# A cross-entropy gradient kernel on one core: whole-block and row transfers change places

## The chip, the core and the metric

The kernel runs on 1 core of one Trainium2 chip. The time is device microseconds of one execution. Four kinds of workers matter here:

- VectorE (DVE in the profile) and ScalarE (ACT) compute on rows that lie in SBUF.
- SyncE (SP) computes nothing; it issues the loads, each when what it waits for is done.
- 16 DMA engines move data between HBM and SBUF. SP and ACT each have a queue on all 16 of them: in the profile q1 is SP's and q10 is ACT's.
- TensorE (PE) and GpSimd (POOL) are used in the first microseconds only.

An instruction of an engine waits until a semaphore has reached a count, and raises one when it ends. A DMA raises its semaphore when its data has landed.

## The reference

For each of 8 x 1024 = 8192 positions there are 8192 float32 logits and one label. The output is the softmax minus the one-hot vector of the label:

```python
logits_max = np.max(logits, axis=-1, keepdims=True)
exp_logits = np.exp(logits - logits_max)
softmax = exp_logits / np.sum(exp_logits, axis=-1, keepdims=True)
one_hot[batch_idx, seq_idx, labels] = 1.0
return (softmax - one_hot).astype(np.float32)
```

Logits (268 MB) are read once and the output (268 MB) is written once.

## The kernel before

**Tiling.** A "row" `t` of the program is a tile of 128 positions, one on each of the 128 SBUF partitions, with 8192 float32 on each: 32 KB per partition, 4.19 MB in all. There are T = 64 rows, numbered from 0. Two rows make a block (G = 2), so B = 32 blocks; block `b` has rows `2b` and `2b+1`. In HBM the two rows of a block lie side by side for each partition, 64 KB in one piece. The tile X in SBUF has three slots (SLOTS = 3) of one block each; block `b` lives in slot `b % 3`, is computed in place there, and is stored from there.

**Steps of a row.** All are written with the helper `run` (its line 76 stands for nearly every instruction in the profile).

- `row_max`: DVE takes the negated maximum of the row (`m <- X`).
- `exponentials`: ACT computes exp(x - max) in place and the sum into `s` (`X <- X,m`, and a short instruction that reads the sum).
- `mark`: two ACT instructions (`away`, then `hot`) put a one-hot row, as bytes, into PSUM. A PSUM buffer is free again when the row two before has been finished.
- `finish`: DVE takes the reciprocal of the sum, and then computes row x reciprocal - one-hot in place (`X <- X,r,hot`). The last row's is cut into two column halves.
- `store`: ACT's queue issues the DMA to HBM.

**Order of the main loop.** For block `b` with rows t0 and t1, DVE runs: maximum of t1, finish of t0, maximum of the next block's first row, finish of t1. The third of these is the look-ahead; it is there when `ORDER[b + 1]` is "r", which holds for every block. ACT runs: exponentials of t1, store of t0, marks of row t0 + 2, exponentials of the next block's first row, store of t1, marks of row t1 + 2. At the end of a turn of the loop SP is given the loads of block `b + 3`. The engines run these lists in order and wait where the semaphores say so.

**Pieces.** Two strings give one letter for each block. `LOADS`: "s" loads each row in two halves of the partitions, one by SP and one by ACT; "r" loads row by row with SP; "w" loads the block with one DMA of SP. `STORES`: "r" stores each row when it is finished. A load waits only for those stores of the block before in its slot that it overlaps (`meets`): a row load for the store of the same row, a whole load for both, and a row load for a whole store if the block was stored whole. Before the change blocks 0 to 2 are loaded as "s", 3 and 4 by rows, 5 to 28 whole, 29 to 31 by rows, and all blocks are stored by rows.

**The end.** After the last block ACT waits until the stores of the last three blocks have landed.

Of the kernel before, what the change touches and what calls it, by code (L numbers as in the profile page):

```python
# [7 lines left out]
P = 128  # L8
G = 2
SLOTS = 3  # L10

LOADS = "sssrrwwwwwwwwwwwwwwwwwwwwwwwwrrr"
STORES = "rrrrrrrrrrrrrrrrrrrrrrrrrrrrrrrr"
ORDER = "rrrrrrrrrrrrrrrrrrrrrrrrrrrrrrrr"


@with_exitstack
def kernel(
# [6 lines left out]
    nc = tc.nc  # L25
# [10 lines left out]
    N, V = x_nv.shape  # L36
    T = N // P
# [4 lines left out]
    o_b = o_nv.rearrange("(b p j) v -> b p j v", p=P, j=G)  # L42
# [4 lines left out]
    X = const.tile([P, SLOTS, G, V], fp32)  # L47
# [16 lines left out]
    with tc.tile_critical():  # L64
        sem = tc.alloc_semaphore
        got = [[sem(f"got{i}{q}") for q in range(4)] for i in range(SLOTS)]
        put = [[sem(f"put{i}{q}") for q in range(4)] for i in range(SLOTS)]
# [3 lines left out]
        def run(engine, waits, counter, method, **operands):  # L71

            waits = list(dict.fromkeys(waits))
            for w in waits[:-1]:
                engine.wait_ge(*w)  # L75
            instruction = getattr(engine, method)(**operands)  # L76
            for w in waits[-1:]:
                instruction._wait_ge(*w)
            step = 16 if method == "dma_start" else 1
            instruction.then_inc(counter, step)  # L80
            count[counter.name] = count.get(counter.name, 0) + step
            return counter, count[counter.name]

        every, rows = slice(0, P), slice(0, G)
        one = [slice(j, j + 1) for j in range(G)]
        halves = [slice(i, P, 2) for i in range(2)]
        quarters = [slice(i, P, 4) for i in range(4)]
        PIECES = {
            "r": [(every, js) for js in one],
            "s": [(ps, js) for js in one for ps in halves],  # L90
            "w": [(every, rows)],
            "h": [(ps, rows) for ps in halves],
            "q": [(ps, rows) for ps in quarters],
        }

        def meets(a, b):
            sets = [[set(range(*d.indices(n))) for d, n in zip(p, (P, G))] for p in (a, b)]
            return all(x & y for x, y in zip(*sets))

        loaded, stored = {}, {}  # L100
        maxed, summed, marked, finished, freed = {}, {}, {}, {}, {}

        def load(b):
            loaded[b] = []
            before = stored.get(b - SLOTS, [])
            for q, piece in enumerate(PIECES[LOADS[b]]):
                ps, js = piece
                free = [w for other, w in before if meets(piece, other)]
                queue = nc.scalar if LOADS[b] == "s" and ps == halves[1] else nc.sync
                w = run(  # L110
# [5 lines left out]
        def store(t):  # L116
            b, j = divmod(t, G)
            stored.setdefault(b, [])
            for q, piece in enumerate(PIECES[STORES[b]]):
                ps, js = piece  # L120
                if js.stop != j + 1:
                    continue
                w = run(
                    nc.scalar, [finished[t]], put[b % SLOTS][q], "dma_start",
                    out=o_b[b, ps, js, :], in_=X[ps, b % SLOTS, js, :],
                )
                stored[b].append((piece, w))

        def row(t):
            return X[:, t // G % SLOTS, t % G, :]  # L130
# [4 lines left out]
        def row_max(t):  # L135
            b, j = divmod(t, G)
            arrived = {w[0].name: w for piece, w in loaded[b] if meets(piece, (every, one[j]))}
            maxed[t] = run(
                nc.vector, arrived.values(), dve, "tensor_reduce",
                out=m[:, t : t + 1], in_=row(t), axis=mybir.AxisListType.X, op=Alu.max, negate=True,  # L140
            )

        def exponentials(t):
            w = run(
                nc.scalar, [maxed[t]], act, "activation",
                out=row(t), in_=row(t), func=Act.Exp, bias=m[:, t : t + 1], scale=1.0,
                accum_out=s[:, t : t + 1],
            )
            summed[t] = w

        def mark(t):
            if t >= T:
                return
            w = run(
                nc.scalar, ([made] if t < G else [freed[t - G]]) + ([marked[t - 1]] if t else []), act, "activation",
                out=away[:], in_=count16[:], func=Act.Abs, bias=at(word, t), scale=1.0,
            )
            marked[t] = run(
                nc.scalar, [w], act, "activation",
                out=hot[:, t % G, :], in_=away[:], func=Act.Relu, bias=at(unit, t), scale=at(minus, t),  # L160
            )

        def finish(t, n=1):
            w = run(nc.vector, [summed[t]], dve, "reciprocal", out=r[:, t : t + 1], in_=s[:, t : t + 1])
            bytes_ = hot[:, t % G, :].bitcast(u8)
            for i in range(n):
                c = slice(i * V // n, (i + 1) * V // n)
                last = run(
                    nc.vector, [marked[t], w] if i == 0 else [], dve, "scalar_tensor_tensor",
                    out=row(t)[:, c], in0=row(t)[:, c], scalar=r[:, t : t + 1], in1=bytes_[:, c],  # L170
                    op0=Alu.mult, op1=Alu.subtract,
                )
            finished[t] = freed[t] = last

        w_raw = run(nc.scalar, [], lab_got, "dma_start", out=lab_raw[:], in_=lab_bp)
        for b in range(SLOTS):
            load(b)
        w = run(nc.gpsimd, [], pool, "memset", ap=ident[:], constant=0.0)
        w_ident = run(
            nc.gpsimd, [w], pool, "affine_select",  # L180
            out=ident[:], in_=ident[:], compare_op=Alu.not_equal, fill=1.0,
# [8 lines left out]
        for j in range(G):  # L190
            w = run(
                nc.tensor, [w_ident, w_lab], pe, "transpose",
                out=lab_ps[:, j, :], in_=lab_f[:, j, :], identity=ident[:],
            )
        w = run(nc.vector, [w], dve, "tensor_copy", out=lab[:], in_=lab_ps)
        w = run(
            nc.vector, [w], dve, "tensor_scalar",
            out=part[:], in0=lab[:], scalar1=2, scalar2=None, op0=Alu.arith_shift_right,
        )
        w_word = run(  # L200
            nc.vector, [w], dve, "tensor_scalar",
            out=word[:], in0=part[:], scalar1=-1.0, scalar2=None, op0=Alu.mult,
        )
        w = run(
            nc.vector, [w_word], dve, "tensor_scalar",
            out=lab[:], in0=lab[:], scalar1=3, scalar2=None, op0=Alu.bitwise_and,
        )
        w = run(
            nc.vector, [w], dve, "tensor_copy", out=minus[:], in_=lab[:]
        )  # L210
        powers = [256.0**k for k in range(4)]
        w = run(
            nc.vector, [w], dve, "tensor_scalar",
            out=unit[:], in0=minus[:], scalar1=0.0, scalar2=powers[0], op0=Alu.is_equal, op1=Alu.mult,
        )
        for k in (1, 2, 3):
            w = run(
                nc.vector, [w], dve, "tensor_scalar",
                out=part[:].bitcast(fp32), in0=minus[:], scalar1=float(k),
                scalar2=powers[k], op0=Alu.is_equal, op1=Alu.mult,  # L220
            )
            w = run(
                nc.vector, [w], dve, "tensor_tensor",
                out=unit[:], in0=unit[:], in1=part[:].bitcast(fp32), op=Alu.add,
            )
        made_dve = run(
            nc.vector, [w], dve, "tensor_scalar",
            out=minus[:], in0=unit[:], scalar1=-1.0, scalar2=None, op0=Alu.mult,
# [8 lines left out]
        for b in range(B):  # L237
            t0, t1 = b * G, b * G + 1
            nxt = t1 + 1
            if ORDER[b] == "b":  # L240
                if t0 not in maxed:
                    row_max(t0)
                    exponentials(t0)
                row_max(t1)
                exponentials(t1)
                finish(t0)
                store(t0)
                mark(t0 + G)
                finish(t1)
                store(t1)  # L250
                mark(t1 + G)
                if b + SLOTS < B:
                    load(b + SLOTS)
                continue
            if t0 not in maxed:
                row_max(t0)
                exponentials(t0)
            row_max(t1)
            finish(t0)
            exponentials(t1)  # L260
            store(t0)
            mark(t0 + G)
            ahead = nxt < T and ORDER[b + 1] == "r"
            if ahead:
                row_max(nxt)
            finish(t1, 1 if t1 + 1 < T else 2)
            if ahead:
                exponentials(nxt)
            store(t1)
            mark(t1 + G)  # L270
            if b + SLOTS < B:
                load(b + SLOTS)
# [33 lines left out]
```

## Time and profile before

| | us |
|---|---|
| median of 3 runs (1248.36 to 1248.45) | 1248.44 |
| the profiled execution | 1248.19 |
| its span in the trace | 1246.4 |
| DVE busy | 1120.1 (90%) |
| ACT busy | 722.7 (58%) |
| one maximum, DVE, x64 | 8.68 |
| one finish of a whole row, DVE, x63 | 8.75 |
| one half of the last row's finish, DVE, x2 | 4.48 |
| one row of exponentials, ACT, x64 | 7.12, and 0.19 for the sum |
| `away` and `hot`, ACT, x64 each | 2.00 and 2.06 |
| one reciprocal, DVE, x64 | 0.15 |
| mean rate of all DMA over the span | 431 GB/s |

How to read the lines that follow. A page line of an engine gives busy time and share of the span. The DMA line cuts the span into 40 slices, 9 for 90% busy or more. A queue line gives packets, megabytes and the time of its packets as a share of 16 engines over the stretch asked for; it counts a packet in full where it starts, so that a short stretch can show over 100%. Packets of 4 bytes that raise semaphores are among the number. A wait line gives who waited for whom: us in total, times, and the longest. A line of a stretch gives its bounds, its length, the busy time of PE, PEld, DVE, ACT and POOL with counts, the clock, and last the DMA share and GB/s. A line of DMA issues ends with the median time from issue to landing.

### The profile page before, as it was taken

To read this page: it belongs to the slowest core of one execution; us is meant where nothing else is said; L and a number is where in the kernel's file an instruction comes from. 1 tells how busy PE (TensorE), PEld (TensorE's weight loads), DVE (VectorE), ACT (ScalarE), POOL (GpSimd) and SP (SyncE) were. 2 spreads that over 40 slices of the span, in tenths; PEclk is the share of its full clock that TensorE was granted. 3 is DMA by queue.
4 is the path that set the end of the run, shared out by engine and by line. 5 is a ranking of instruction groups with operands and counts; after the bars stand their busy time and mean duration, and the time that the engine had idled before them with its cause. 6 is when DMAs were issued, how large, how long until landed. Compare 5 with 4: busy or idle time off the path is not lost.

```text
span 1246.4 us, 805 instructions
## 1 busy us (share of the span) xinstructions
PE 0.4 (0%) x2; PEld 0.3 (0%) x2; DVE 1120.1 (90%) x207; ACT 722.7 (58%) x257; POOL 2.3 (0%) x7
## 2 busy tenths in 40 slices
PE   0000000000000000000000000000000000000000
PEld 0000000000000000000000000000000000000000
DVE  5999997888988889888899889998989988899995
ACT  2866664557555565555655556655556565566662
POOL 0000000000000000000000000000000000000000
DMA  9999999999999999999999999999999999999998
GB/s 401 416 430 435 437 432 446 422 430 434 433 434 444 439 419 446 423 429 437 431 442 436 422 432 431 433 438 449 423 423 437 435 445 428 426 434 434 432 430 385
DMA packets 15125, 536.98 MB, mean 431 GB/s; under 512 B 1776, under 2 KB 1776, under 8 KB 1808
## 3 DMA queue, kind: packets, MB, share of 16 engines
q10 hardware_dynamic: 9744, 281.09, 52.3%
q1 hardware_dynamic: 5376, 255.86, 47.5%
q14 instruction: 5, 0.04, 0.0%
HBM read 268.50 MB, written 268.44 MB: 431 GB/s over the span
## 4 chain that ended last, share of the span: by engine, by line
DMA 59%; DVE 26%; issue 11%; ACT 3%; DVEq 0%; ACTq 0%; SPq 0%
DMA X<-in_logits_dram 33%; DMA out_dram<-X 26%; DVE X L76 15%; DVE m L76 10%; ACT X L76 2%; DVEq L64 0%; DVE r L76 0%; ACT hot L76 0%; ACT away L76 0%; ACTq L76 0%; DVEq L75 0%; ACTq L301 0%; SPq L64 0%
## 5 line engine op out<-in xcount | busy, mean ns | idle before, releaser
L76 ACT ACTIVATE X<-X,m 128x8192 f32<-128x8192 f32 x64 | 455.8, 7122 | 365.3 <-DVE m L76 365.3
L76 DVE TENSOR_REDUCE m<-X 128x1 f32<-128x8192 f32 x64 | 555.6, 8682 | 105.6 <-DMA X<-in_logits_dram 105.6
L76 DVE SCALAR_TENSOR_TENSOR X<-X,r,hot 128x8192 f32<-128x8192 f32 (+1 forms) x65 | 560.0, 8616 | 3.8 <-ACT hot L76 1.6
L76 ACT ACTIVATE away<-count,word 128x2048 bf16<-128x2048 int16 x64 | 128.1, 2001 | 127.0 <-DVE X L76 127.0
L76 ACT ACTIVATE hot<-away,unit,minus 128x2048 int32<-128x2048 bf16 x64 | 131.9, 2062 | 2.1
L76 ACT ACTIVATION_READ_ACCUMULATOR X<-X,m 128x1 f32 x64 | 11.9, 186 | 0.0
L76 DVE RECIPROCAL r<-s 128x1 f32<-128x1 f32 x64 | 9.8, 154 | 0.0
L76 ACT ACT_TABLE_LOAD x1 | 1.3, 1283 | 5.4 <-issue 5.4
L76 DVE CAST lab_f<-lab_raw 32x256 f32<-32x256 int32 x1 | 0.5, 511 | 2.8 <-DMA lab_raw<-in_labels_dram 2.8
L76 POOL IOTA count<- 128x2048 int16 x1 | 1.8, 1823 | 0.0
L76 DVE TENSOR_TENSOR unit<-unit,part 128x64 f32<-128x64 f32 x3 | 0.7, 224 | 0.1
L76 DVE CAST lab<-hot 128x64 int32<-128x64 f32 x1 | 0.2, 225 | 0.5 <-PE hot L76 0.5
L76 DVE TENSOR_SCALAR part<-minus 128x64 f32<-128x64 f32 x3 | 0.6, 195 | 0.1
L76 PE MATMUL hot<-ident,lab_f 32*128 32x32 f32 x2 | 0.4, 299 | 3.3 <-DVE lab_f L76 3.3
L76 PEld LDWEIGHTS hot<-ident,lab_f 32*128 32x128 f32 x2 | 0.3, 193 | 3.3 <-DVE lab_f L76 3.3
L76 DVE TENSOR_SCALAR word<-part 128x64 f32<-128x64 int32 x1 | 0.2, 197 | 0.0
L76 DVE TENSOR_SCALAR part<-lab 128x64 int32<-128x64 int32 x1 | 0.2, 195 | 0.0
L76 DVE TENSOR_SCALAR unit<-minus 128x64 f32<-128x64 f32 x1 | 0.2, 195 | 0.0
L76 DVE TENSOR_SCALAR lab<-lab 128x64 int32<-128x64 int32 x1 | 0.2, 195 | 0.0
L76 DVE CAST minus<-lab 128x64 f32<-128x64 int32 x1 | 0.2, 195 | 0.0
L76 DVE TENSOR_SCALAR minus<-unit 128x64 f32<-128x64 f32 x1 | 0.2, 195 | 0.0
L76 POOL TENSOR_SCALAR_AFFINE_SELECT ident<-ident 32x32 f32<-32x32 f32 x1 | 0.2, 202 | 0.1
(5 smaller groups left out, 0.5 us busy)
## 6 DMA issues: line engine op xcount, KB each, us to landing
out_dram<-X ACTq DMA_DIRECT2D x64, 4096.0 KB, 30.2
X<-in_logits_dram SPq DMA_DIRECT2D x10, 4096.0 KB, 27.7
X<-in_logits_dram SPq DMA_DIRECT2D x6, 2048.0 KB, 32.8
X<-in_logits_dram ACTq DMA_DIRECT2D x6, 2048.0 KB, 37.2
X<-in_logits_dram SPq DMA_DIRECT2D x24, 33.3
lab_raw<-in_labels_dram ACTq DMA_DIRECT2D x1, 64.0 KB, 1.8
```

Of the source, the lines that this page charges most:

```text
L76: instruction = getattr(engine, method)(**operands)
```

## The change

Blocks 5 to 25 are now loaded row by row (they were loaded whole); blocks 26 to 28 stay whole. Blocks 3 to 24 are stored whole, with one DMA when the second row is finished; all other blocks are stored by rows. The new letter "n" in `ORDER` for blocks 2 to 24 takes the look-ahead out of the blocks 1 to 23: DVE runs the two maxima and then the two finishes. Of the last two rows, 62 and 63, each is finished in two column halves, and each half is stored by its own DMA as soon as it is finished: row 62's by SP, row 63's by ACT. Two kinds of pieces that no block used are taken out.

```diff
-LOADS = "sssrrwwwwwwwwwwwwwwwwwwwwwwwwrrr"
-STORES = "rrrrrrrrrrrrrrrrrrrrrrrrrrrrrrrr"
-ORDER = "rrrrrrrrrrrrrrrrrrrrrrrrrrrrrrrr"
+LOADS = "sssrrrrrrrrrrrrrrrrrrrrrrrwwwrrr"
+STORES = "rrrwwwwwwwwwwwwwwwwwwwwwwrrrrrrr"
+ORDER = "rrnnnnnnnnnnnnnnnnnnnnnnnrrrrrrr"
...
+        sides = [slice(i * V // 2, (i + 1) * V // 2) for i in range(2)]
...
         def store(t):
             b, j = divmod(t, G)
             stored.setdefault(b, [])
+            if t >= T - G:
+                for i, cs in enumerate(sides):
+                    w = run(
+                        nc.sync if t == T - G else nc.scalar, [sides_done[t][i]], put[b % SLOTS][G * j + i],
+                        "dma_start", out=o_b[b, every, one[j], cs], in_=X[every, b % SLOTS, one[j], cs],
+                    )
+                    stored[b].append(((every, one[j]), w))
+                return
...
-        def finish(t, n=1):
+        def finish(t):
             w = run(nc.vector, [summed[t]], dve, "reciprocal", out=r[:, t : t + 1], in_=s[:, t : t + 1])
             bytes_ = hot[:, t % G, :].bitcast(u8)
-            for i in range(n):
-                c = slice(i * V // n, (i + 1) * V // n)
+            sides_done[t] = []
+            for i, c in enumerate(sides if t >= T - G else [slice(0, V)]):
                 last = run(
...
+                sides_done[t].append(last)
...
-            finish(t1, 1 if t1 + 1 < T else 2)
+            finish(t1)
```

More of the change, by code (lines that the diff above doesn't have):

```diff
@@ L86 @@
         halves = [slice(i, P, 2) for i in range(2)]
-        quarters = [slice(i, P, 4) for i in range(4)]
+        sides = [slice(i * V // 2, (i + 1) * V // 2) for i in range(2)]
         PIECES = {
@@ L91 @@
             "w": [(every, rows)],
-            "h": [(ps, rows) for ps in halves],
-            "q": [(ps, rows) for ps in quarters],
         }
@@ L98, in meets @@
             return all(x & y for x, y in zip(*sets))
-        loaded, stored = {}, {}
+        loaded, stored, sides_done = {}, {}, {}
         maxed, summed, marked, finished, freed = {}, {}, {}, {}, {}
```

## The prediction

> **What bounds the kernel now.** I read the page from its top. Part 1 gives the engines, part 2 the DMA line, part 3 the queues (q1 is SP's: most loads; q10 is ACT's: all stores and six half-row loads).
>
> ```profile
> PE 0.4 (0%) x2; PEld 0.3 (0%) x2; DVE 1120.1 (90%) x207; ACT 722.7 (58%) x257; POOL 2.3 (0%) x7
> ...
> DMA  9999999999999999999999999999999999999998
> ...
> q10 hardware_dynamic: 9744, 281.09, 52.3%
> q1 hardware_dynamic: 5376, 255.86, 47.5%
> ```
>
> The two queues add up to 99.8% of 16 engines' span. DVE is busy 90%, but waits; the lists of waits say for what (the first line from all engines, the others from SP's own queue):
>
> ```profile
> DVE m L76 <- DMA X<-in_logits_dram: 105.6, 26, 9.2
> ...
> SPq L76 <- DMA out_dram<-X: 645.1, 34, 68.3
> SPq L75 <- DMA out_dram<-X: 511.0, 24, 21.9
> ```
>
> DVE waits for loads, loads wait for stores to land, and the DMA engines never rest: the kernel is bound by bytes through 16 engines. So an order of transfers can only gain where the engines rest, and lose where it makes them rest. Two questions follow: does the packet shape change the rate, and where are the holes?
>
> Rate. The DMA answer for 240 to 1090 us, where every load but one is whole (64 KB packets) and every store a row (32 KB packets):
>
> ```profile
> q1 hardware_dynamic: 3214, 186.06, 50.6%
> q10 hardware_dynamic: 6253, 182.36, 49.7%
> ```
>
> A 64 KB packet takes 0.506 x 16 x 850 / (186.06 MB / 65,536 B) = 2.424 us, a 32 KB one 0.497 x 16 x 850 / (182.36 MB / 32,768 B) = 1.215 us, which is 0.006 us per 64 KB dearer. Reading a share to 0.1 point makes each good to 0.1%. In 1100 to 1195 us, where both directions go by rows, the mean is 434 GB/s, against 433 here.
>
> Who goes first. The same answer for 552 to 577 us, with both queues full:
>
> ```profile
> q1 hardware_dynamic: 116, 7.60, 70.3%
> q10 hardware_dynamic: 112, 3.15, 29.1%
> ```
>
> 116 packets of one queue beside 112 of the other: they take turns by packet, so the queue with packets twice as long gets two thirds. Now that is the loads; after the change it is the stores.
>
> Holes. The stretches at the end (DMA share and GB/s are last), and three answers on DMA issues, one each for the stores of rows 61, 62 and 63 (numbered from 0), issued at 1206.8, 1224.2 and 1233.2:
>
> ```profile
> 1206.00:1222.00 16.00, 0.00 (x0) 0.00 (x0) 15.96 (x4) 10.68 (x3) 0.00 (x0) 1.00 1.00 432
> 1222.00:1226.00 4.00, 0.00 (x0) 0.00 (x0) 3.96 (x3) 0.60 (x2) 0.00 (x0) 1.00 0.65 279
> 1226.00:1240.00 14.00, 0.00 (x0) 0.00 (x0) 7.18 (x2) 0.00 (x0) 0.00 (x0) 1.00 1.05 449
> ```
> ```profile
> out_dram<-X ACTq DMA_DIRECT2D x1, 4096.0 KB, 18.6
> ```
> ```profile
> out_dram<-X ACTq DMA_DIRECT2D x1, 4096.0 KB, 11.1
> ```
> ```profile
> out_dram<-X ACTq DMA_DIRECT2D x1, 4096.0 KB, 11.9
> ```
>
> The one hole before the last landing is at 1222 to 1226: row 61's store is nearly out and row 62's comes too late. They land at 1225.4, 1235.3 and 1245.1. The last spacing, 9.76 us, is a row's bare transfer; the one before is 9.96.
>
> **The change, part by part.**
>
> *Last rows in column halves.* Row 62's finish runs from 1215.45 and takes 8.75 us; a half takes 4.48 (the last row's two halves in the trace), so its first half is issued at 1219.95 instead of 1224.24, while row 61's store is still moving, and the hole closes. Gain, from below: the landing row shows 9.96 - 9.76 = 0.2 us (the engine that ends last loses least). From above: the shares show 4 x 0.35 - 14 x 0.05 = 0.7 us, a mean over the engines. I take 0.7, the row that counts all engines. Row 62 goes by SP's queue, whose last load is issued at 1173.2, so nothing stands before it; two more DMAs cost ACT or SP an issue of about 0.34 us each, beside the transfer backlog. The 16 KB packets: by the 0.006 above for each halving, 256 packets are cut, 16 per engine, 0.1 us at most. Two halved finishes instead of one on DVE: 2 x 4.48 - 8.75 = 0.2 us, and DVE's last half need only be out one half-transfer, 4.9 us, before the end: by 1245.1 - 0.6 - 1.4 - 4.9 = 1238.2 (1.4 is row 62's 11.1 - 9.76 from issue to landing beyond the transfer), while it is ready at 1233.2. That is 5 us of cover.
>
> *Packet shapes.* 21 blocks are loaded in 32 KB packets instead of 64 (168 pairs per engine), 22 stored in 64 KB instead of 32 (176). If a long store packet saves what a long load packet does: 168 x 0.006 - 176 x 0.006, nothing. If it saves nothing: +1.0 us. A long store packet is not in the trace; by the two stretches (433 and 434 GB/s, 0.2% apart) the middle, 850 us, could move by 2 us either way. I take 0: at 32 KB both directions cost 1.21 to 1.22, as the row-by-row stretch with its 50.6% and 49.9% shows too.
>
> *Number of transfers.* 22 stores fewer, 21 loads more, 2 more at the end: 112 instead of 111. SP issues 21 more, at 0.33 us, while it waits hundreds of us. Nothing.
>
> *No look-ahead in the middle.* Blocks 1 to 23 no longer put the next row's maximum between their two finishes. DVE's instructions stay the same: per block 2 x 8.68 + 2 x 8.75, with the reciprocals some 34.9 us (the chain's pace is 17.45 per row). The second finish needs its exponentials; they start when its maximum ends and take 7.12 + 0.19 beside the first finish's 8.75 + 0.15. The first finish's exponentials lie beside the second maximum, 8.68. Cover is 1.4 to 1.6 us; if ACT were late, DVE would lose that much per block. ACT's marks (2.0 + 2.1 per row) fall under the second finish and the next maximum: no wait.
>
> *Whole stores, loads by rows.* This decides. A block now leaves at its end only, and both row loads into its slot wait for that one landing. A block is 16.78 MB / 433 GB/s = 38.75 us of DMA, 19.4 each way; DVE needs 34.9, so DVE runs ahead until it waits for loads, 3.85 us per block. Behind the waiting second maximum stand both finishes and the whole store. Ledger from E, the moment when block b's store is issued: it gets two thirds and is out at E + 29.1. DVE needs 8.68 + 2 x 8.75 = 26.2 us from a block's second row landing to its store, and landing costs some 0.6; so the loads of b+1, whose store goes at E + 38.75, end at E + 38.75 - 26.8 = E + 11.9. From then until E + 29.1 the loads of b+2 get a third: 5.7 of their 19.4 us. When store b lands, 13.7 us of loads are still queued. Restarting the next loads costs 11.1 - 9.76 + 0.33 = 1.7 us, hidden by these 13.7. If it were not hidden: 1.7 us per turn.
>
> The Trainium skill, "DMA: Bandwidth & Descriptors", section "Anatomy of one DMA", puts about 2.0 us of fixed time on each DMA, most of it the wait for the write's receipt before the semaphore fires. By that rule and with no cover, 22 whole stores that must land before a reload would add 22 x 2.0 = 44 us (1292 in all), an estimate from that page; the trace hides such times already, with 111 transfers at 99.8% busy.
>
> *Sum.* The profiled execution took 1248.19 (span 1246.4 and 1.8 around it). -0.7 + 0.1 + 0 = -0.6: 1247.6. The median of the runs stands 0.25 above the profiled one, so 1247.8.
>
> **Rivals.**
>
> *A. The queues run dry at whole stores* (slower). If at a landing fewer than 1.7 us of loads are queued and no other store is out, the engines rest for the difference. The steady ledger leaves 13.7, but the start is thinner: block 3 is the first whole store, with DVE still behind (it runs without waits from 36 to 167 us in the trace, so stores come as late as they can). Two such turns at full price cost 3.4 us: 1251; all 22 cost 37: 1285. Against: at the start the next stores are queued at 17.45 us per row, with 30 us to land each, so one covers the other.
>
> *B. Long store packets are slower than long load packets.* Nothing shows them. By the bounds above +1 to +2: 1249 to 1250; from 2.6% of a packet (0.063 us x 176 = 11 us) it would be 1259, with no row for it.
>
> *C. DVE is late at the end.* With stores favoured, loads come later, and DVE has the last eight rows to do at 17.45 each after its last wait (at 1084.5 now). Past the 5 us of cover, each us costs one: with 8 us of delay 1251. Against: the change loads blocks 26 to 28 whole, while stores go by rows from 25 on, so loads have two thirds again there.
>
> *D. The hole does not close,* because row 61's store lands sooner, or the halves come late: 1248.4 to 1248.6.
>
> *E. Faster by more:* long store packets cheaper by over 0.6%, 176 x 0.015 = 2.6 us: 1245.2. The trace has a difference of 0.2% by shape only.
>
> **How the numbers follow.** Forecast 0.55 (1247.2 to 1248.3), D 0.15, B 0.08 (a quarter of it past 0.2%), A 0.12, C 0.06 (half), E 0.04. 0.2% is 2.5 us, about what a measurement of this kernel can tell from no change. Slower by more: 0.12 + 0.02 + 0.03 = 0.17; faster by more: 0.04; within: 0.79. The range leaves out E below (1246.2) and most of A and the tails of B and C above (1251.0).
>
> **What would show it.** Right: the two queues again near 99.8%; no slice of the DMA line under 9 but the last; 1222 to 1226 at a share near 1.0; a whole store from issue to landing in 29 to 33 us; DVE's waits for loads again about 100 us in all, now at second maxima; with only loads by rows and whole stores queued, q10 at two thirds. Wrong: DMA share under 0.97 in stretches that begin at a whole store's landing (A), lower GB/s at a full share (B), DVE ending after 1238 (C).

## The result and the profile after

The changed kernel takes 1303.28 us (median of 4 runs, 1292.94 to 1306.15) against 1248.45 before: a ratio of 1.0424, 95% interval 1.0398 to 1.0450. 1247.8 was predicted. Its profiled execution took 1306.15 us with a span of 1304.4, 58 us more than the 1246.4 of before.

The page of the changed kernel, engines, DMA line, rates and queues:

```profile
PE 0.4 (0%) x2; PEld 0.3 (0%) x2; DVE 1119.7 (86%) x208; ACT 722.8 (55%) x257; POOL 2.3 (0%) x7
...
DMA  9999999999995999999996999999889999999999
GB/s 404 417 433 434 434 433 419 429 425 408 411 434 241 436 417 425 420 427 403 417 421 249 422 442 408 424 416 417 355 368 435 433 427 423 433 433 434 433 432 393
...
q10 hardware_dynamic: 6576, 276.89, 50.1%
q1 hardware_dynamic: 8688, 260.05, 47.0%
```

The compute engines do the same work in the same time. The DMA line has three holes (5, 6, and 8 8), and between them the rate is often under 430 GB/s. The queues add up to 97.1% of a longer span, where they added up to 99.8%.

The answer on DMA for 240 to 1000 us, in which whole stores and loads by rows run:

```profile
q10 hardware_dynamic: 2620, 152.83, 47.9%
q1 hardware_dynamic: 5233, 152.08, 47.6%
```

A 64 KB store packet takes 0.479 x 16 x 760 / (152.83 MB / 65,536 B) = 2.498 us in the mean, a 32 KB load packet 0.476 x 16 x 760 / (152.08 MB / 32,768 B) = 1.247. Before, the long ones (loads then) took 2.424 and the short ones (stores) 1.215. At those times the two queues would have needed 46.5% and 46.4% here, so slower packets cost 2.6% of 760 us, 20 us. The share that is missing, 4.5%, is 34 us in which engines had nothing to do. Together 54 of the 58 us: the loss has two parts. The slower packets are a minority: the median long store packet of this stretch still takes 2.418 us, and one in six takes over 2% more than that, 2.9 us in the mean.

Stretches of the changed kernel around the first hole (DMA share and GB/s are last), and the timeline there:

```profile
393.00:396.00 3.00, 0.00 (x0) 0.00 (x0) 3.00 (x1) 3.00 (x1) 0.00 (x0) 1.00 0.54 229
396.00:410.00 14.00, 0.00 (x0) 0.00 (x0) 13.96 (x4) 7.20 (x4) 0.00 (x0) 1.00 0.13 54
410.00:412.00 2.00, 0.00 (x0) 0.00 (x0) 2.00 (x1) 1.93 (x1) 0.00 (x0) 1.00 1.25 524
```
```profile
348.30 8.69 DVE L76 TENSOR_REDUCE m<-X 128x1 f32<-128x8192 f32 x1 [25.54 <-DMA X<-in_logits_dram]
...
374.73 0.34 ACTq L76 DMA_DIRECT2D out_dram<-X  x1
...
409.63 0.34 ACTq L76 DMA_DIRECT2D out_dram<-X  x1
```

A share of 0.13 is 2 of 16 engines (three at first, then one). For 14 us these finish the store issued at 374.7 (block 8's) while the others are idle: the next loads into its slot wait for that landing, the other engines have done all earlier loads, and the next store is issued at 409.6 only. A DMA signals its landing sixteen times, once for each engine. In the trace of before the sixteen signals of one transfer are at most 7.0 us apart, mostly 1 to 4. Here those of a load of block 10 are 34.9 us apart: thirteen come at 375 to 377 us and three, from engines that had to do this load beside the store, at 403 to 410. The wait of 25.54 us at 348.3 is the same at a load: the second row of block 8 is late on some engines, and DVE has nothing else in its list.

The hole at 685 to 702 looks the same (three late signals, the last 35.8 us after the first). In the one at 930 to 952 five engines are late, and the share falls to 0.44 only. DVE's waits for loads grew from 105.6 us to 164.2:

```profile
DVE m L76 <- DMA X<-in_logits_dram: 164.2, 21, 25.8
```
```profile
SPq L76 <- DMA out_dram<-X: 1180.2, 35, 68.2
```

(The first line is from all engines, the second from SP's queue.) At the end the predicted hole did close. The stretches of the changed kernel that answer to 1222 to 1240 of before:

```profile
1280.00:1284.00 4.00, 0.00 (x0) 0.00 (x0) 3.96 (x3) 0.81 (x2) 0.00 (x0) 1.00 0.96 414
1284.00:1298.00 14.00, 0.00 (x0) 0.00 (x0) 7.52 (x2) 0.00 (x0) 0.00 (x0) 1.00 1.01 431
```

### The profile page after: what moved, and what is told of

Its sections match the earlier page's. It is cut to its first block, busy times and chain, and to the rows that moved or that the text cites. A ratio compares the mean times of both kernels' runs of the same rounds, so it can differ in the third digit from the quotient of the medians.

```text
span 1304.4 us, 785 instructions
## 1 busy us (share of the span) xinstructions
PE 0.4 (0%) x2; PEld 0.3 (0%) x2; DVE 1119.7 (86%) x208; ACT 722.8 (55%) x257; POOL 2.3 (0%) x7
## 4 chain that ended last, share of the span: by engine, by line
DMA 50%; DVE 33%; issue 9%; another core or an unknown queue 6%; ACT 1%; DVEq 0%; SPq 0%; ACTq 0%
DMA X<-in_logits_dram 28%; DMA out_dram<-X 22%; DVE X L76 18%; DVE m L76 14%; ACT X L76 1%; DVE r L76 0%; DVEq L64 0%; ACT hot L76 0%; ACT away L76 0%; SPq L76 0%; ACTq L76 0%; DVEq L75 0%; ACTq L308 0%; SPq L64 0%
## 5 line engine op out<-in xcount | busy, mean ns | idle before, releaser
L76 DVE TENSOR_REDUCE m<-X 128x1 f32<-128x8192 f32 x64 | 554.6, 8680 | 164.2 <-DMA X<-in_logits_dram 164.2
```

## The experiments

Times are medians; each ratio is to the kernel before, run on the same chip. Edits are against the changed kernel, where nothing else is said. Letters of `LOADS`, `STORES` and `ORDER` are given as runs: "w x22" is 22 times "w". Times of the sixteen landing signals are read from the traces' semaphore events.

### Which part of the change

**The tail alone.** The kernel before with the column halves of rows 62 and 63.

```diff
-LOADS = sss, r x23, w x3, rrr   STORES = rrr, w x22, r x7   ORDER = rr, n x23, r x7
+LOADS = sss, rr, w x24, rrr     STORES = r x32              ORDER = r x32
```

> The kernel before with the column halves of the last two rows alone. All theories: the hole at the end closes and nothing else moves, 1247.6 to 1248.3 us, against 1248.4 before. Over 1250 would mean that the tail has a part in the loss.

Measured: 1248.43 us, ratio 1.0000 (0.9990 to 1.0010). The hole closes (its stretches end in DMA share and GB/s), and no gain shows:

```profile
1222.00:1226.00 4.00, 0.00 (x0) 0.00 (x0) 3.96 (x3) 1.01 (x2) 0.00 (x0) 1.00 0.94 401
1226.00:1240.00 14.00, 0.00 (x0) 0.00 (x0) 7.72 (x2) 0.00 (x0) 0.00 (x0) 1.00 1.01 431
1240.00:1246.60 6.60, 0.00 (x0) 0.00 (x0) 0.00 (x0) 0.00 (x0) 0.00 (x0) 1.00 0.49 209
```

The rest moved to the last stretch (0.49, where before had 0.57): without the hole the engines no longer restart together, their last landing signals are 2.1 us apart (0.2 before), and the last engine ends where it ended.

**Rows stored again.** Loads, order and tail as changed.

```diff
-STORES = rrr, w x22, r x7
+STORES = r x32
```

> The changed kernel with all stores by rows again; loads by rows and no look-ahead in the middle as changed. Theory 'long turns' (a 64 KB store packet beside a 32 KB load packet lets a DMA engine that is a little behind fall far behind, and a whole block's landing waits for the last engine) and theory 'one landing' (reloads wait for a whole block, whatever the packets) both put the loss on the whole stores: 1247 to 1250 us. If the loads by rows, or the missing look-ahead, were the cause, it would stay near 1300.

Measured: 1248.61 us, 1.0002 (0.9993 to 1.0011). The loads by rows and the missing look-ahead cost nothing. All of the loss hangs on the whole stores.

**Look-ahead back, whole stores kept.**

```diff
-ORDER = rr, n x23, r x7
+ORDER = r x32
```

> The changed kernel with the look-ahead back in all blocks; long whole stores and loads by rows as changed. If the missing look-ahead has a part in the loss (a second maximum that waits for its load holds both finishes and the store): 1260 to 1290 us. 'Strays': no part, 1290 to 1306 us.

Measured: 1302.85 us, 1.0440 (1.0404 to 1.0476), as without it. The order of DVE's work has no part.

### Length of packets, or what is waited for

**Two row stores at the block's end.** The moment of the store and the waits stay; the packets are 32 KB.

```diff
-STORES = rrr, w x22, r x7
+STORES = rrr, e x22, r x7
...
+            if STORES[b] == "e":
+                if j == 1:
+                    for q, js in enumerate(one):
+                        w = run(
+                            nc.scalar, [finished[t]], put[b % SLOTS][q], "dma_start",
+                            out=o_b[b, every, js, :], in_=X[every, b % SLOTS, js, :],
+                        )
+                        stored[b].append(((every, rows), w))
+                return
```

> The changed kernel, but where it stores a whole block with one DMA, two row stores (32 KB packets) are issued together at the same moment, and both row loads of the next block in the slot wait for both: same order, same waits, shorter packets. 'Long turns' and 'slow long store packets': the loss goes, 1247 to 1255 us, with packets at 1.21 us and a DMA share of 99% or more in the middle. 'One landing': it stays, 1290 to 1306 us.

Measured: 1250.03 us, 1.0013 (1.0004 to 1.0023). This is the run that decides. DMA for 240 to 1000 us:

```profile
q1 hardware_dynamic: 5623, 167.77, 51.3%
q10 hardware_dynamic: 5522, 161.02, 49.1%
```

The engines are busy throughout, a packet takes 0.513 x 16 x 760 / (167.77 MB / 32,768 B) = 1.218 us. The common landing costs 1.6 us; the rest goes with storing the block as one DMA of 64 KB packets (the length of the packets and the number of DMAs change together here). "One landing" falls as a cause by itself.

**Long packets both ways.**

```diff
-LOADS = sss, r x23, w x3, rrr
+LOADS = sss, rr, w x24, rrr
```

> The changed kernel with blocks 5 to 28 loaded whole again, so loads and stores both move 64 KB packets. 'Long turns': turns are equal again, an engine that is behind loses half as much of its load's rate, so most of the loss goes, 1250 to 1270 us. 'One landing': the reload still waits for the whole store, and the whole load lands later than its first row would, 1300 us or more. 'Slow long store packets' (the mean 64 KB store packet grew from the nominal 2.42 to 2.50 us in the middle): the packets stay slow, about 1270 us.

Measured: 1286.54 us, 1.0289 (1.0254 to 1.0324); the runs lie between 1280.1 and 1300.0. Equal turns save a third of the loss, not most of it: "long turns" expected at most 1270, and the other two theories missed too. So it isn't only that a store has two thirds. DMA for 240 to 1000 us:

```profile
q1 hardware_dynamic: 2624, 153.09, 49.6%
q10 hardware_dynamic: 2669, 156.04, 48.4%
```

By the same working a load packet takes 2.58 us and a store packet 2.47: here the loads are the slower ones.

**Short packets, unequal turns.** Two row stores at the end (32 KB), loads in column halves (16 KB).

```diff
-LOADS = sss, r x23, w x3, rrr     STORES = rrr, w x22, r x7
+LOADS = sss, rr, c x21, w x3, rrr STORES = rrr, e x22, r x7
...
+            if LOADS[b] == "c":
+                free = [w for _, w in before]
+                for q, (js, cs) in enumerate([(js, cs) for js in one for cs in sides]):
+                    w = run(nc.sync, free, got[b % SLOTS][q], "dma_start",
+                        out=X[every, b % SLOTS, js, cs], in_=x_b[b, every, js, cs])
+                    loaded[b].append(((every, js), w))
+                return
```

> As the kernel with two row stores at a block's end, but blocks 5 to 25 are loaded in column halves, 16 KB packets. So the store packet is again twice the load packet, loads again get a third beside stores, and reloads wait for the whole block; only no packet is longer than 32 KB. Theory 'unequal turns' (the loss comes from stores having two thirds): 1280 us or more. Theory 'strays' (an engine out of step with the others is slowed only by 64 KB packets beside long stores, lags more and more, and the landing waits for it): 1249 to 1254 us, packets at 0.61 and 1.21 us.

Measured: 1273.86 us, 1.0199 (1.0179 to 1.0219), between the two expectations. DMA for 240 to 1000:

```profile
q1 hardware_dynamic: 10985, 162.99, 51.4%
q10 hardware_dynamic: 5472, 159.39, 49.1%
```

No hole here (100.5% together); the packets are slow: 0.628 us for 16 KB, where the undisturbed column halves at the end take 0.611 each in the trace of the tail alone, and 1.228 for 32 KB. So a store packet twice as long as the load packet is bad at half the length too. "Strays", which blamed 64 KB alone, falls in that form.

**Long loads, short stores, common landing.**

```diff
-LOADS = sss, r x23, w x3, rrr   STORES = rrr, w x22, r x7
+LOADS = sss, rr, w x24, rrr     STORES = rrr, e x22, r x7
```

> Two row stores (32 KB packets) at a block's end and reloads that wait for both, with blocks 5 to 28 loaded whole in 64 KB packets: the mix of the kernel before with the common landing of the changed one. If only long store packets throw the engines out of step: 1249 to 1255 us. If long packets in either direction do so once nothing but whole blocks are waited for: 1270 us or more.

Measured: 1254.88 us, 1.0049 (1.0032 to 1.0065). The mix of before bears the common landing, at 6 us.

### The traffic by itself

Four kernels that only move the blocks: loads of two blocks and stores of two blocks always in flight, no store waiting for a load but for the first. Each ran once.

```diff
+        for q, (ps, js) in enumerate(PIECES[STORE]):
+            before = [last_store[b % 2, q]] if (b % 2, q) in last_store else [last_load[2, 0]]
+            last_store[b % 2, q] = run(nc.scalar, before, put[b % 2][q], "dma_start",
+                out=o_b[b, ps, js, :], in_=X[ps, 2, js, :])
```

> Transfers alone, with nothing computed: every block loaded and stored once (the output is not the gradient; all stores come from one slot), two blocks of loads and two of stores always in flight, no store waits for a load. Stores in 64 KB packets, loads in 32 KB, as in the middle of the changed kernel. Theory 'the traffic itself is slow' (64 KB store packets beside loads contend, whoever waits): while both queues run, packets take 2.50 us and 1.25 us as in the changed kernel or more, about 420 GB/s. Theory 'drift and waits' (packets are slow only because the engines are thrown out of step by waits and restarts): 2.42 and 1.215 us, 433 GB/s, and no hole.

> The same with 32 KB store packets and 64 KB load packets, as in the middle of the kernel before. Both theories: 433 GB/s, packets 1.215 and 2.42 us.

> The same with 64 KB packets both ways. 'The traffic itself is slow': packets of 2.5 us or more, 410 to 425 GB/s. 'Drift and waits': 2.42 us, 433 GB/s.

> The same with 32 KB packets both ways. Both theories: 433 GB/s, packets 1.215 us.

Measured, GB/s in 100 to 600 us: 435, 425, 434, 433, in this order. Totals: 1269.23, 1266.16, 1247.93, 1247.16 us. The mix of the changed kernel runs at full rate; its packets take 2.42 and 1.22 us. "The traffic itself is slow" falls for it. The second was a miss for both theories: the mix of the kernel before ran at 425, with long load packets of 2.49 us (0.674 x 16 x 500 / (141.76 MB / 65,536 B), from the line below), and its landing signals drew apart from 0.7 to 7 us. And the first ended late for a reason that the rate hides: the sixteen landing signals of a transfer, up to 0.7 us apart until 320 us, were 10 apart at 640 and 23 at 950, because one engine fell behind (the other fifteen signals lie within 0.8 us). Its lag stayed at 23 us from then on, when the stores were nearly done and loads ran alone. With equal packets the spread didn't keep growing: at 64 KB (third) it went from 0.6 to 4.5 us by 260 us and stayed there, at 32 KB (fourth) it never passed 0.8.

```profile
q1 hardware_dynamic: 2435, 141.76, 67.4%
```

### Engines put out of step on purpose

Four small loads ahead, which go to a few engines only (16 packets of 24 KB); the first loads of blocks wait for them. Both kernels ran once, on another chip than the four above.

```diff
+        for n, slot, j in ((2, 0, 0), (2, 0, 1), (4, 1, 0), (8, 1, 1)):
+            w_nudge = run(
+                nc.sync, [], nudge, "dma_start",
+                out=X[:n, slot, j, : 3 * V // 4], in_=x_b[B - 1, :n, j, : 3 * V // 4],
+            )
```

> The run of transfers alone with 32 KB packets both ways, which went at 433 GB/s with no slow packet; new: four small loads first, on 2, 2, 4 and 8 of the partitions, which go to the lowest-numbered engines only and put engines 0 to 7 out of step by some 0.9 to 3.7 us (24 KB each, by 1.215 us per 32 KB). Theory 'out of step is slow' (an engine out of step with the others is slowed by itself, whatever put it there, and stays so): under 430 GB/s in 100 to 600 us, landings spread by more and more us. Theory 'long or unequal packets are slow, and only while they run': 433 GB/s, the spread stays at some 4 us.

Measured: 1256.10 us, 9 more than without. DMA for 100 to 600 us:

```profile
DMA packets 7432, 216.67 MB, mean 433 GB/s; under 512 B 820, under 2 KB 820, under 8 KB 820
```

The small loads put the engines further apart than the 0.9 to 3.7 us expected: the first load's signals are 9.8 us apart. They are at most 9.4 us apart for a load at 49 us and 9.3 at 1153. The 9 us are paid once.

> The run of transfers alone with 64 KB stores and 32 KB loads (435 GB/s in 100 to 600 us, one engine lagging by 23 us at the end, 1269 us), with the same four small loads first. 'Out of step is slow': 425 GB/s or less in 100 to 600 us, and a total of 1275 us or more. Otherwise as without the small loads.

Measured: 1368.39 us, 99 more than without. DMA for 100 to 600 us, nudged, then not nudged:

```profile
DMA packets 4723, 205.69 MB, mean 411 GB/s; under 512 B 528, under 2 KB 528, under 8 KB 528
...
q10 hardware_dynamic: 2338, 136.45, 66.2%
q1 hardware_dynamic: 2385, 69.24, 33.9%
```
```profile
DMA packets 4970, 217.32 MB, mean 435 GB/s; under 512 B 559, under 2 KB 559, under 8 KB 559
...
q10 hardware_dynamic: 2493, 145.56, 67.2%
q1 hardware_dynamic: 2477, 71.76, 33.3%
```

The long packet takes 0.662 x 16 x 500 / (136.45 MB / 65,536 B) = 2.54 us instead of 2.42, the short one 1.28 instead of 1.22, and the landing signals of a load are 24 us apart at 241 us, 51 at 555 and 110 at 947. Nothing is computed and no store waits for a load. Again the first load's signals are 9.6 us apart. So with 64 KB stores beside 32 KB loads a difference between the engines slows packets and grows; with 32 KB both ways it stays as it is. The pair shows one way to slow packets that needs neither compute nor waits. That it is the whole cause in the changed kernel isn't shown: with 64 KB both ways, where the traffic alone ran at 434 GB/s, packets in the kernel were slow too.

**In the kernel.** The same small loads ahead of the kernel before, of the one with row stores (1248.6), and of the one with two row stores at the end (1250.0). The loads of blocks 1 and 2 wait for them.

> The kernel before, with nothing changed but the same four small loads ahead of its own, and the loads of blocks 1 and 2 waiting for them. 'Out of step is slow': 1255 us or more, with slower packets. Otherwise 1250 to 1253 us: the 3.7 us of the most loaded engines.

> The kernel with the changed loads and order but all stores by rows (1248.6 us), with the four small loads ahead that put engines 0 to 7 out of step. In traffic alone with 32 KB packets these cost 9 us at the start and nothing after it. 'Out of step is slow only with long or unequal packets': 1256 to 1259 us, the lag stays as it is, 433 GB/s in 450 to 950 us. 'Out of step is slow in the kernel whatever the packets' (which the rows after five whole stores, 428 GB/s, speak for): 1265 us or more, under 430 GB/s.

> The kernel with two row stores at a block's end (1250.0 us), with the same four small loads ahead. 'Only with long or unequal packets': 1257 to 1261 us, 433 GB/s in 450 to 950 us. 'In the kernel whatever the packets': 1270 us or more, since here a landing also waits for the whole block.

Measured: 1265.05 us (1.0124, 1.0107 to 1.0140), 1262.48 (1.0115, 1.0098 to 1.0132) and 1263.79 (1.0124, 1.0109 to 1.0140). DMA of the second for 450 to 950 us:

```profile
DMA packets 7439, 216.52 MB, mean 433 GB/s; under 512 B 830, under 2 KB 830, under 8 KB 830
```

The third has 433 there too, and the lags hardly change (a load's signals 4.5 us apart at 456 and 5.0 at 941 in the second, 2.8 and 3.1 in the third). Both totals lie between what the two theories expected. Most of the second's 14 us are paid at the two ends: its first 30 us run at 313 GB/s instead of 403 (6 us), its last 60 at a share of 0.88 instead of 0.94 (4 us). That is more than expected of the small loads, but in the middle short packets bear engines out of step in the kernel too, where no long store came before. The kernel before, with 64 KB loads, came out as "out of step is slow" expected, with load packets of 2.44 us in the mean instead of 2.42; but the middle explains only about 4 of its 16 us (431 GB/s in 240 to 1090 us instead of 433).

### How fast it builds up, and how long it lasts

**Five long stores.**

```diff
-STORES = rrr, w x22, r x7
+STORES = rrr, w x5, r x24
```

> The changed kernel with long whole stores in blocks 3 to 7 alone (5 in place of 22). A loss in proportion to the long packets: 5/22 of 55, 12 us, 1261 us. 'Strays' whose lag builds up over some ten blocks until the engines run dry (the first hole of the changed kernel is at 393 us, when block 9's store goes): lag but no hole, 1248 to 1253 us.

Measured: 1283.98 us, 1.0254 (1.0209 to 1.0299); the runs lie between 1273.5 and 1305.3. Both expectations were far too low. The last long store has landed by 360 us; DMA for 600 to 1000 us, where both ways go by rows, here and then in the kernel with row stores throughout:

```profile
DMA packets 5854, 171.39 MB, mean 428 GB/s; under 512 B 653, under 2 KB 653, under 8 KB 653
...
X<-in_logits_dram SPq DMA_DIRECT2D x18, 4096.0 KB, 51.9
```
```profile
DMA packets 5827, 173.56 MB, mean 434 GB/s; under 512 B 641, under 2 KB 641, under 8 KB 641
...
X<-in_logits_dram SPq DMA_DIRECT2D x18, 4096.0 KB, 27.7
```

The same instructions with the same packets, 240 us after the last long one, run 1.4% slower, and the landing signals of a load spread from 7 us at 409 to 19 at 902.

**With one drain.**

```diff
+                free += [w for d in (10, 11) for _, w in stored[d]] if b == 12 else []
...
-            if b + SLOTS < B:
-                load(b + SLOTS)
+            for c in {9: [], 10: [], 11: [12, 13, 14]}.get(b, [b + SLOTS]):
+                if c < B:
+                    load(c)
```

> The kernel with five whole stores (blocks 3 to 7), with one drain: the loads of blocks 12, 13 and 14 are held until the stores of blocks 9 to 11 have landed too, so that all engines stop and start together, once. Without it, rows both ways went at 428 GB/s in 450 to 950 us, long after the last long packet, against 433 where no long store came before. 'Out of step is slow, and stays until the engines stop': 433 GB/s and landings within 2 to 3 us of each other after the drain. If something else lasts: 428 again. The total is no test, the drain itself costs 30 to 60 us.

Measured: 1290.76 us, 1.0336 (1.0286 to 1.0386). The drain did what it should: the landing signals go from 26 us apart before it to 0.2 at 485 us. But they grow again, to 3 at 678 and 11 at 995, and 600 to 1000 us runs at 426 GB/s:

```profile
DMA packets 5838, 170.28 MB, mean 426 GB/s; under 512 B 640, under 2 KB 640, under 8 KB 640
```

So "stays until the engines stop" falls: something else than the lag itself lasts. The issue-to-landing times of loads and stores (51.9 and 34.0 us, with the drain 36.9 and 46.4) are not those of the kernel with row stores throughout (27.7 and 52.0), so the queues stand differently to each other. That doesn't sort the cases, though: the nudged kernel with two row stores at the end has 34.3 and 34.0 and kept 433. What lasts is open.

## Why the prediction was wrong

- **What bounds the kernel.** Right: bytes through the DMA engines, and any rest of theirs is time. That accounts for the loss, 34 us of rest and 20 of slower packets. One reading was off: of the 112 packets of q10 beside 116 of q1, 16 are the 4-byte ones of a landing, so it was 96 beside 116. That the queues take turns shows better in the traffic alone, where 67.2% and 33.3% go to packets of 64 and 32 KB.
- **Last rows in column halves, -0.7 us.** Not confirmed: measured 0.0, but with an interval of 1.2 us either way, which has 0.7 in it. The stretches speak for little or nothing: the hole closed and its rest moved to the last 6.6 us. Of the two ends given, 0.2 from the landing row and 0.7 from the shares, I took the one that counts all engines. But the end is set by the last engine, and that one had hardly waited.
- **Packet shapes, 0 within 2 us.** Wrong. The times were read where the engines are in step, and taken as a property of the packet. Long store packets took 3.0% and the loads beside them 2.6% more in the mean, 20 us in all. Rival B's price for 2.6% on the stores alone, 11 us, was near their part of it (0.074 us x 176 = 13); it left out the loads, and was set aside because no row showed it. No row of before could.
- **Number of transfers, no look-ahead.** Right: 1248.61 us with both and with row stores.
- **Whole stores, loads by rows.** This step failed: the cover that was to hide every landing. The ledger has one store queue and one load queue, with 13.7 us of loads left at a landing, and so no rest; the engines rested 34 us. There are sixteen of each queue. Most engines ran out of work while three to five were still on the old, and every wait is for the last of sixteen. With two row stores in place of the whole one the cover held (the same waits cost 1.6 us). The ledger's 0.6 us for a landing stands in no row; in the trace of before the last signal comes 0.35 us after the last data packet's end, too small a difference to matter. The share of two thirds that I read for stores makes it worse, and the ledger had the number: an engine that has loads left when a store arrives does them at a third of the rate, so its lag grows. (That this is how the 34.9 us came about is worked out, not shown.) The Trainium skill, "DMA: Bandwidth & Descriptors", section "Why a DMA increments its semaphore by 16 and not by 1", says that the engines of a DMA finish independently and only the full count means landed. The trace agrees, with sixteen signals up to 35.8 us apart; I had read past it.
- **Rival A** named the place, the engines dry at whole stores, and at its full price 1285. Its mechanism, a thin queue at the start and 1.7 us of restart per turn, is not what happened: there were three holes of 9 to 14 us. As for the 2.0 us of fixed time per DMA: the Trainium skill, "DMA: Bandwidth & Descriptors", section "Anatomy of one DMA", describes them for DMAs issued by GpSimd, while these are issued by SP and ACT. The kernel with two row stores at the end waits for its landing at every turn and loses 1.6 us in all, so whatever this time is here, it stays hidden.
- **Rival C** did not occur: the late loads showed in the middle, and DVE closed the tail as predicted.

Shown: the loss comes with storing a block in 64 KB packets by one DMA instead of in 32 KB packets by two (1303.3 against 1250.0 with the same waits), it is 20 us of slow packets and 34 of idle engines, and the idle ones wait for three to five late ones. In this mix of packets engines that were put out of step got slower packets and drifted apart with no compute at all (411 against 435 GB/s, one execution each). Open: which of an engine's packets become slower and why, why the same mix ran at full rate for 600 us when it wasn't nudged, why 64 KB both ways is slow in the kernel and not by itself, and why rows stay slow after five long stores, even after a drain. No version beat the kernel before.

## What to carry to other kernels

A saturated DMA is sixteen queues, not one: when a wait covers a whole block, ask what the slowest engine does, and read the spread of the landings beside the mean share. The safest packets here were short and of the same length both ways: two row stores issued at one moment cost 1.6 us where one store of the same bytes cost 55. It is no law, since the kernel before does as well with loads twice as long. Before trusting that a transfer pattern is at its limit, push a few engines out of step for some microseconds and see whether the lag stays or grows.

## What the runs showed of the hardware

- The mean time of a packet isn't fixed by its length. In traffic alone 64 KB stores took 2.42 us, and 2.54 after small loads had put the first load's landing signals 9.6 us apart; the median was 2.418 both times.
- With 64 KB stores beside 32 KB loads a lag grew (to 110 us in the nudged traffic); with 32 KB both ways a lag of 9.4 us was still 9.3 us after 1100 us. Each is one execution.
- The mix of the kernel before has the weakness too: by itself it ran at 425 GB/s, and inside the kernel at 433.
- Closing the hole at 1222 us gained 0.0 us, within 1.2: with the hole the engines end in step (last signals 0.2 us apart), without it 2.1 us apart.
